# The two parts of x^T and the tile of ones allocated first in their pool

## The chip, the core and the metric

The kernel runs on one core of a Trainium2 chip. The metric is the device time of one execution in microseconds (us); the kernel before takes 1495.61 us, the median of three runs (1495.11 to 1495.95).

## What is computed

Two transformer-like blocks act on 256 tokens of width 1024, in float32. Cut to the products that matter here:

```python
def swiglu(h, wg, wu, wd):
    return (silu(h @ wg) * (h @ wu)) @ wd          # 1024 -> 2816 -> 1024

# first block: FFN, mixer (convolution + gated linear attention), FFN, embedding
h = h + 0.5 * swiglu(rmsnorm(h), ...)              # f1
z = rmsnorm(h) @ w_in                              # mixer input
h = h + concat(y_conv, y_gla) @ w_out
h = h + 0.5 * swiglu(rmsnorm(h), ...)              # f2
h = h + sigmoid(rmsnorm(h) @ w_gate) * (p @ w_proj)
# second block, two layers: FFN, attention (layer 0) or spatial gating (layer 1), FFN
x = x + g1 * swiglu(modulate(rmsnorm(x)), ...)     # f3, f5
x = x + g2 * mix(modulate(rmsnorm(x)))             # attention; spatial gating
x = rmsnorm(x + g3 * swiglu(modulate(rmsnorm(x)), ...))   # f4, f6
```

Nearly all of the arithmetic is a product of normed activations, 256 x 1024, with a weight.

## The kernel before

A float32 value is split in two float32r parts, H (a cast on ScalarE) and L (the remainder, a subtraction on VectorE). A product of two such pairs is three matmuls: H by H, L by H, H by L. The weights come from HBM as a stream of 1 MB entries, in the order of use; `Stream` issues the transfers on SP's queue, three entries ahead (tile `raw`), and splits halves of an entry into tiles `wh` and `wl`, eight of each.

The normed activations stand transposed, features on the partitions, in two tiles `xh` and `xl` of 128 partitions by 2 token tiles by 8 k-tiles by 128 tokens: 8192 bytes in each partition. `norm_T` writes them (L571 transposes, L498 and L499 split), once for each of the stages; everything that multiplies normed activations reads them. Two forms do:

- `mm3` (L490 to L492) with 128 tokens of x^T as the stationary operand and 512 columns of a weight as the moving one: the first two chunks of each FFN, and the products of the mixer, the embedding gate, attention and spatial gating. The same lines also serve the products whose stationary operand is another tile: the gated values `g` of the FFNs (`down`), and `oHL`, `sHL`, `yHL`, `cHL`, `pTHL`.
- `mmT` (L692), called by `chunkT`, with 128 columns of a weight as the stationary operand and all 256 tokens of one k-tile of x^T as the moving one, read as two runs of 128 values that lie 4096 bytes apart: the other nine chunks of each FFN and some of the mixer's input.

Every matmul loads its own stationary operand. Tile `ones_r` is the stationary operand of 18 warming products at the start (L421) and of one small sum in attention.

A list scheduler sets the order of the instructions on each engine, from priorities that the program gives (`ahead`, `spawn`, `tick`); `attention` and `sgu` set VectorE's order by hand. Memory is handed out pool by pool and, inside a pool, tile by tile in the order of the program, each tile rounded up to 32 bytes. The pool of the constants begins at byte 106,624 of each partition, a multiple of 64. Before `ones_r`, `xh` and `xl` come two tiles `h` of 4096 bytes, `kc` of 1536, `cols` of 1508 (377 columns, rounded to 1536) and `neghalf` of 32. So `ones_r`, `xh` and `xl` begin at 117,920, 118,432 and 126,624: each 32 bytes past a multiple of 64. `wh`, `wl`, `raw`, `g` and every other float32r tile begin at multiples of 64, and the slices of them that the matmuls read do too.

Of the kernel before, what the change touches and what calls it, by code (L numbers as in the profile page):

```python
# [10 lines left out]
F32R = mybir.dt.float32r  # L11
# [5 lines left out]
PSUM = bass.MemoryType.PSUM  # L17

P = 128
# [11 lines left out]
# buffers of each tag; tiles of one tag are handed out in the order of the program,  # L31
# so chains of work that run beside each other have tags of their own
# [6 lines left out]
# how many down-projection steps a tile does alone at the end of an FFN,  # L39
# and how many gate/up chunks the first tile does alone at its start  # L40
TAIL = 3
HEAD = 2
# taps of the convolution issued per us of the tensor engine's work
CONV_RATE = 3.0
# taps of each channel that the tensor engine takes
# [4 lines left out]
# how far ahead of its place in the program the scheduler may take a chain's work  # L50
# [6 lines left out]
# ---------------------------------------------------------------- weights  # L57
# Each entry of the stream is [128, 2048]: two blocks [128, 1024] of a weight.
#   "c": four k-tiles x 512 columns (two of each 1 MB entry make 8 k-tiles)
#   "d": two k-tiles x 1024 columns  # L60
#   "ada": transposed, two blocks of 128 columns of a modulation vector x 1024 rows
# [33 lines left out]
# the modulation vectors of the second block (shift, scale, gate of each part)  # L95
# are made while these FFNs run: layer, vectors
# [30 lines left out]
# columns of the packed per-partition constants  # L127
# [17 lines left out]
# columns of the shape-only constants  # L145
K_ID, K_LOW, K_UP, K_END, K_CAUSAL = 0, 128, 256, 384, 384
# rows
# [3 lines left out]
class Stream:  # L151
    """The weights, in order: DMA ahead, then split into H + L, float32r parts
    whose sum is the float32 weight."""
# [21 lines left out]
    def pump(self, now=False, n=0):  # L175
        """splits what there is room for, or n halves of an entry"""
# [38 lines left out]
class Task:  # L215
    """A chain of work given as a generator. What it yields is how much work of the
    tensor engine (us) is to be issued before the chain goes on, or a task to wait for."""
# [7 lines left out]
class Kernel:  # L225
# [25 lines left out]
    # -------------------------------------------------------------- order of issue  # L251
    @contextmanager
    def ahead(self, n):
        """the scheduler takes what is traced inside as if it were n instructions earlier"""
        tc = self.tc
        at = tc.cur_priority
        tc.cur_priority = at - n
        yield
        tc.cur_priority += n

    def pin(self, i):
        """what `after` is given later does not go before i on its engine"""
        self.pins[i.ins.engine] = i.ins
# [8 lines left out]
    def hold(self, on):  # L272
        """no weights are split while a chain runs that the tensor engine waits for"""
        self.held = on
        if not on:
            self.ws.pump()
# [31 lines left out]
    def tick(self, us):  # L308
        """so much work of the tensor engine has been issued"""
        self.pe += us  # L310
        if self.conv_q:
            self.conv_due += us * self.conv_rate
            while self.conv_q and self.conv_due >= 1.0:
                self.conv_due -= 1.0
                self.conv_q.pop(0)()
        if self.busy:
            return
        self.busy = True
        while self.heap and self.heap[0][0] <= self.pe:
            self._advance(heapq.heappop(self.heap)[2])  # L320
        self.busy = False
# [10 lines left out]
    # -------------------------------------------------------------- tiles  # L332
# [11 lines left out]
    def junk(self):  # L344
        """what only its sum is needed of"""
        return self.sp.tile([P, 512], BF16, tag="junk", name=self.nm("junk"), bufs=1)
# [7 lines left out]
    def psa(self, s, i, shape):  # L354
        """a bank of the accumulators, where none is in use"""
        return self.pacc.tile(shape, F32, tag=f"acc{i // 2}{i % 2}", name=self.nm(s))
# [10 lines left out]
    # -------------------------------------------------------------- start  # L367
    def setup(self):
        nc, a = self.nc, self.a
        self.h = [self.cpool.tile([P, D], F32, name=f"h{t}") for t in range(NT)]  # L370
# [4 lines left out]
        self.ones_r = self.cpool.tile([P, P], F32R, name="ones_r")  # L375
        nc.gpsimd.memset(self.ones_r.bitcast(F32), 1.0)
        self.xh = self.cpool.tile([P, NT, KT, P], F32R, name="xh")
        self.xl = self.cpool.tile([P, NT, KT, P], F32R, name="xl")
# [3 lines left out]
        # the first function of the scalar engine, of the table that the others here are in too  # L382
# [12 lines left out]
    def start(self):  # L395
        """x^T of the input, and the first weights"""
# [17 lines left out]
        # products of ones, that nothing reads, bring the tensor engine to its full clock  # L414
# [20 lines left out]
    # -------------------------------------------------------------- modulation  # L435
# [18 lines left out]
    def ada_end(self, layer, v, s):  # L454
        """a modulation vector: in columns, the gates in rows"""
# [30 lines left out]
    # -------------------------------------------------------------- pieces  # L486
# [8 lines left out]
    def split(self, dst, src):  # L495
        """dst = (H, L), src float32 in SBUF or PSUM"""
# [10 lines left out]
    def square(self, x, s):  # L507
        """sum of squares / 1024 of half a row"""
# [4 lines left out]
    def rstd(self, ss, t):  # L513
        """1/rms from the two halves' sums; with four, also that of 1/rms times what the other two are of"""
# [6 lines left out]
        if n == 2:  # L521
            # (s2 / (s1 + eps) + eps)^-1/2 (s1 + eps)^-1/2 = (s2 + eps (s1 + eps))^-1/2
# [6 lines left out]
    def residual(self, t, hf, gate, scale, keep):  # L529
        """h + gate * acc, half a row: in h, or keeps h"""  # L530
# [16 lines left out]
    def norm_T(self, t, ss, a, b=None):  # L547
        """x^T of tile t: (h / rms) * a + b, features on partitions, as H and L"""
# [62 lines left out]
    def finish(self, t, scale=None, gate=None, a=None, b=None, row=None, upd=None, last=False):  # L611
        """h += ..., then the norms that lead to the next x^T"""
# [38 lines left out]
    # -------------------------------------------------------------- projections  # L651
    def chunk(self, key, t, ps):
        """ps[128 tokens, 512] = x @ chunk, over 8 k-tiles"""
# [8 lines left out]
    def by_tile(self, name, cs, pss=None):  # L662
        """several chunks, all of them for one token tile before the next"""
# [6 lines left out]
    def chunkT(self, key, banks):  # L670
        """the transpose of x @ chunk: 128 columns on the partitions, all tokens;
        bank [128, 2, 256] i of the two has column blocks i and i + 2"""
# [14 lines left out]
    def mmT(self, out, w, x, first, last):  # L687
        """out[columns, tokens] += w^T x; the groups of a bank share its first start"""
# [8 lines left out]
    def down(self, t, units, first, last):  # L697
        """acc[t] += x[k-tile]^T @ weight[k-tile] over units (key, half, x)"""
# [10 lines left out]
    def down2(self, name, order, xs, fin):  # L709
        """the product with a weight of four entries: the first token tile ends early enough  # L710
        for its norms to run beside the rest of the second's"""
# [14 lines left out]
    def ffn(self, name, fin):  # L726
# [39 lines left out]
        # first chunks: a token tile at a time, so that the first need not wait for the second  # L766
# [25 lines left out]
    # -------------------------------------------------------------- first block: mixer  # L792
    def mixer_load(self):
        nc, a = self.nc, self.a
        yield 30.0
        # the 16 columns of the gate's low rank, padded to the array's width
# [15 lines left out]
    def conv_taps(self, b):  # L812
        """depthwise causal convolution of a block of channels, a tap at a time"""
# [16 lines left out]
    def conv_diag(self):  # L830
        """diagonal matrices of the last taps, for each block of channels"""
# [9 lines left out]
    def conv_pe(self, bs):  # L841
        """the last taps of some blocks of channels, as products with diagonal matrices"""
# [41 lines left out]
    def gla_gates(self, zt):  # L884
        """decays of the gated linear attention, channels on the partitions"""
# [42 lines left out]
    def gla_scores(self, banks, gates):  # L928
        """q, k with their decays; scores inside the chunks of 64; k of the chunks' end by tokens"""
# [17 lines left out]
        for t in range(NT):  # L947
# [6 lines left out]
            for e in range(2):  # L954
                # a bank for each half of the array's rows
# [12 lines left out]
    def gla_state(self, c):  # L968
        """S_{c+1} = exp(cum_end) * S_c + k_end^T v"""
# [77 lines left out]
    def mixer(self, fin):  # L1047
# [4 lines left out]
        # a * sigmoid(b): the first half of the channels a token tile at a time  # L1052
# [33 lines left out]
        # low rank of the gates  # L1086
# [56 lines left out]
    # -------------------------------------------------------------- first block: per-layer embedding  # L1143
# [37 lines left out]
    # -------------------------------------------------------------- differential attention  # L1181
    def attn_load(self):
        """bias of each head by distance, and lambda"""
# [21 lines left out]
        # lambda_init + e0 - e1, negated  # L1205
# [8 lines left out]
    def attn_qk(self, c, t, ps):  # L1214
        """q or k of four heads: rms norm of the groups of 64, channels on the partitions"""
# [22 lines left out]
    def attn_softmax(self, hf, pr, t, lane):  # L1238
        """p0 - lambda * p1 of two heads, transposed"""
# [22 lines left out]
        for i in range(2):  # L1262
            # the bias is stored from the last key to the first
# [40 lines left out]
    def attn_values(self, hf, t, deps):  # L1304
# [12 lines left out]
        # squares scaled by 2^-40; a sum beyond float32's range gives 1/rms = 0  # L1317
# [62 lines left out]
    # -------------------------------------------------------------- spatial gating  # L1380
# [84 lines left out]
    # -------------------------------------------------------------- all of it  # L1465
# [57 lines left out]
# ---------------------------------------------------------------- host: layout only  # L1523
# [6 lines left out]
def pack(inputs):  # L1530
# [21 lines left out]
    def ch(dst, parts, half):  # L1552
        # parts: column blocks of a [1024, n] weight; four k-tiles of it
# [75 lines left out]
    # bucket of the distance n - 127  # L1629
# [38 lines left out]
```

## Time and profile before

| | |
|---|---|
| device time, median of 3 | 1495.61 us |
| span of the profiled execution | 1494.0 us |
| around the span (median less span; the profiled execution's own device time is not listed apart) | 1.6 us |
| TensorE (PE) busy | 1467.5 us, 98% |
| weight loads (PEld) busy | 1300.4 us, 87% |
| VectorE (DVE), ScalarE (ACT) busy | 1086.6 and 782.3 us, 73% and 52% |
| DMA, mean | 232 GB/s |

A matmul's record runs from its start to the end of its last result, so neighbouring records overlap, and neither "busy" nor the mean of one record tells how fast matmuls follow each other. That is read from their starts: of two rows of the list in order, the difference of the start times over the number of matmuls between them. Names of operands are written out<-in; in the name of a matmul the moving operand stands first and the stationary one second.

### The profile page before, as it was taken

To read this page: it belongs to the slowest core of one execution; us is meant where nothing else is said; L and a number is where in the kernel's file an instruction comes from. 1 tells how busy PE (TensorE), PEld (TensorE's weight loads), DVE (VectorE), ACT (ScalarE), POOL (GpSimd) and SP (SyncE) were. 2 spreads that over 40 slices of the span, in tenths; PEclk is the share of its full clock that TensorE was granted. 3 is DMA by queue.
4 is the path that set the end of the run, shared out by engine and by line. 5 is a ranking of instruction groups with operands and counts; after the bars stand their busy time and mean duration, and the time that the engine had idled before them with its cause. 6 is when DMAs were issued, how large, how long until landed. Compare 5 with 4: busy or idle time off the path is not lost.

```text
span 1494.0 us, 23272 instructions
## 1 busy us (share of the span) xinstructions
PE 1467.5 (98%) x9256; PEld 1300.4 (87%) x9256; DVE 1086.6 (73%) x1693; ACT 782.3 (52%) x1238; POOL 55.2 (4%) x60
## 2 busy tenths in 40 slices
PE   8999999999999999999999999999999999999998
PEld 6999989779999878999776889998899988889997
DVE  6876569978775688775678788866987658685554
ACT  6544566265444584444586554446544455554442
POOL 1000000100000000000122100000000000000000
PEclk9999999999999999999999999999999999999999
DMA  8887544138776448786445388863899846276550
GB/s 311 335 310 267 191 149 183 64 134 319 296 290 233 148 157 320 301 315 216 155 141 199 116 330 347 325 249 127 312 350 335 300 145 235 105 291 225 205 204 29
DMA packets 52332, 346.06 MB, mean 232 GB/s; under 512 B 5912, under 2 KB 8704, under 8 KB 11776
## 3 DMA queue, kind: packets, MB, share of 16 engines
q1 hardware_dynamic: 52224, 344.58, 62.2%
q8 instruction: 72, 1.18, 0.3%
q14 instruction: 36, 0.29, 0.1%
HBM read 343.47 MB, written 1.09 MB: 231 GB/s over the span
## 4 chain that ended last, share of the span: by engine, by line
PE 80%; DVE 9%; ACT 4%; DMA 3%; issue 2%; POOL 2%; SPq 0%; POOLq 0%; DVEq 0%; ACTq 0%
PE gu L692 39%; PE acc L492 9%; PE acc L490 9%; PE acc L491 9%; DVE wl L197 4%; DMA raw<-wpack 3%; PE gu L491 2%; PE gu L492 2%; PE gu L490 2%; ACT wh L196 1%; DVE cacc L824 1%; PE xT L571 1%; POOL rn L504 1%; ACT s L1275 1%; PE cv L848 1%
## 5 line engine op out<-in xcount | busy, mean ns | idle before, releaser
L197 DVE TENSOR_TENSOR wl<-raw,wh 128x1024 fp32r<-128x1024 f32 x490 | 588.2, 1221 | 244.2 <-ACT wh L196 243.4
L196 ACT CAST wh<-raw 128x1024 fp32r<-128x1024 f32 x490 | 502.2, 1050 | 396.4 <-DMA raw<-wpack 159.4
L692 PE MATMUL gu<-xh,wh 128*128 128x256 f32 x1728 | 484.3, 281 | 1.8 <-DVE g L736 1.1
L692 PE MATMUL gu<-xl,wh 128*128 128x256 f32 x1728 | 482.2, 279 | 0.0
L692 PE MATMUL gu<-xh,wl 128*128 128x256 f32 x1728 | 482.1, 279 | 0.0
L692 PEld LDWEIGHTS gu<-xh,wh 128*128 128x128 f32 x1728 | 324.8, 188 | 5.1 <-DVE g L736 1.7
L692 PEld LDWEIGHTS gu<-xl,wh 128*128 128x128 f32 x1728 | 324.8, 188 | 2.4
L692 PEld LDWEIGHTS gu<-xh,wl 128*128 128x128 f32 x1728 | 324.8, 188 | 0.0
L492 PE MATMUL acc<-wl,g 128*128 128x512 f32 x528 | 207.2, 392 | 0.0
L490 PE MATMUL acc<-wh,g 128*128 128x512 f32 x528 | 207.2, 394 | 0.0
L491 PE MATMUL acc<-wh,g 128*128 128x512 f32 x528 | 206.5, 391 | 0.0
L447 DVE SCALAR_TENSOR_TENSOR raw<-raw,cact 128x1024 f32<-128x1024 f32 x144 | 171.7, 1219 | 17.9 <-DMA raw<-wpack 17.8
L492 PEld LDWEIGHTS acc<-wl,g 128*128 128x128 f32 x528 | 99.1, 188 | 22.4
L491 PEld LDWEIGHTS acc<-wh,g 128*128 128x128 f32 x528 | 99.1, 188 | 20.8 <-DVE g L499 1.2
L490 PEld LDWEIGHTS acc<-wh,g 128*128 128x128 f32 x528 | 99.2, 188 | 18.8
L734 ACT ACTIVATE s<-gu 128x256 f32<-128x256 f32 x108 | 40.7, 384 | 78.5 <-PE gu L692 78.3
L490 PE MATMUL gu<-wh,xh 128*128 128x512 f32 x192 | 76.7, 400 | 1.8 <-ACT wh L196 1.4
L492 PE MATMUL gu<-wl,xh 128*128 128x512 f32 x192 | 76.1, 398 | 1.4 <-DVE wl L197 1.4
L491 PE MATMUL gu<-wh,xl 128*128 128x512 f32 x192 | 76.3, 398 | 0.5 <-DVE xl L499 0.5
L736 DVE TENSOR_TENSOR g<-gu,s 128x256 f32<-128x256 f32 x108 | 44.6, 420 | 30.1 <-ACT s L734 29.5
L504 POOL TENSOR_TENSOR rn<-nv,neghalf 128x1 f32<-128x1 f32 (+1 forms) x22 | 20.1, 912 | 1244.6 <-DVE nv L518 1025.8
L498 ACT CAST g<-g 128x256 fp32r<-128x256 f32 x108 | 43.3, 407 | 38.1 <-DVE g L736 37.3
(308 smaller groups left out, 1623.6 us busy)
## 6 DMA issues: line engine op xcount, KB each, us to landing
raw<-wpack SPq DMA_DIRECT2D x316, 1024.0 KB, 4.9
gate<-grow SPq DMA_DIRECT2D x6, 512.0 KB, 4.2
row<-rows SPq DMA_DIRECT2D x5, 512.0 KB, 5.7
bias<-fd SPq DMA_DIRECT2D x16, 128.0 KB, 4.1
raw<-wpack SPq DMA_DIRECT2D x2, 512.0 KB, 7.1
out<-h SPq DMA_DIRECT2D x4, 256.0 KB, 2.2
h<-x SPq DMA_DIRECT2D x2, 256.0 KB
h<-x SPq DMA_DIRECT2D x1, 512.0 KB
```

The source lines that it names most:

```text
L196: self.last = k.after(nc.scalar.copy(out=h, in_=raw[:, u, :]))
L197: k.after(nc.vector.tensor_sub(out=l, in0=raw[:, u, :], in1=h.bitcast(F32)))
L447: self.after(nc.vector.scalar_tensor_tensor(out=raw[:, u, :], in0=raw[:, u, :], scalar=1.0, in1=self.cact, op0=ALU.mult, op1=ALU.mult, acc ...
L490: nc.tensor.matmul(out, lhsT=xh, rhs=wh, start=first, stop=False)
L491: nc.tensor.matmul(out, lhsT=xl, rhs=wh, start=False, stop=False)
L492: nc.tensor.matmul(out, lhsT=xh, rhs=wl, start=False, stop=last)
L498: self.nc.scalar.copy(out=dst[0], in_=src),
L504: self.nc.gpsimd.tensor_tensor(out=r, in0=v, in1=self.neghalf[:, :n], op=ALU.pow)
L571: self.last_T = nc.tensor.transpose(ps[:, i, :], xn[hf][:, i * P : (i + 1) * P], self.ident)
L692: nc.tensor.matmul(out, lhsT=ww, rhs=xx, start=first and n == 0, stop=last and n == 2, skip_group_check=True)
L734: nc.scalar.activation(s, b[:, 0, :], AF.Silu)
L736: nc.vector.tensor_mul(out=y, in0=b[:, 1, :], in1=s)
```

## The change

In `setup`, the three tiles are allocated first in the pool; nothing else differs but comments.

```diff
     def setup(self):
         nc, a = self.nc, self.a
+        self.xh = self.cpool.tile([P, NT, KT, P], F32R, name="xh")
+        self.xl = self.cpool.tile([P, NT, KT, P], F32R, name="xl")
+        self.ones_r = self.cpool.tile([P, P], F32R, name="ones_r")
         self.h = [self.cpool.tile([P, D], F32, name=f"h{t}") for t in range(NT)]
...
         nc.gpsimd.memset(self.neghalf, -0.5)
-        self.ones_r = self.cpool.tile([P, P], F32R, name="ones_r")
         nc.gpsimd.memset(self.ones_r.bitcast(F32), 1.0)
-        self.xh = self.cpool.tile([P, NT, KT, P], F32R, name="xh")
-        self.xl = self.cpool.tile([P, NT, KT, P], F32R, name="xl")
```

Now `xh` begins at 106,624, `xl` at 114,816 and `ones_r` at 123,008, all multiples of 64; `h` at 123,520 and 127,616, `kc` at 131,712, `cols` at 133,248 and `neghalf` at 134,784, multiples of 64 as before. From `cact` (134,816) on every address is the same, and the pools before and behind are where they were. The order of the instructions on all five engines and the semaphores that they wait for are the same, row for row, but for the numbers in the names of the tiles `h`, `xh`, `xl` and `ones_r`; no instruction is added, removed or moved, and none has another shape.

## Rows read from the trace of the kernel before

**Rows 1.** Page: engines' busy us, shares, instructions; granted clock in 40 slices.

```profile
span 1494.0 us, 23272 instructions
...
PE 1467.5 (98%) x9256; PEld 1300.4 (87%) x9256; DVE 1086.6 (73%) x1693; ACT 782.3 (52%) x1238; POOL 55.2 (4%) x60
...
PEclk9999999999999999999999999999999999999999
```

**Rows 2.** Stretches (from:to us): length, busy us (instructions) by engine, clock, DMA, GB/s.

```profile
57.30:200.00 142.70, 142.70 (x1003) 133.02 (x1004) 93.35 (x131) 73.15 (x123) 1.07 (x2) 1.00 0.67 248
850.00:1050.00 200.00, 199.05 (x1304) 180.20 (x1303) 156.68 (x228) 105.59 (x161) 2.88 (x3) 1.00 0.71 268
```

**Rows 3.** Chain of waits, first FFN's start: start us, us, what.

```profile
22.55 7.44 DMA raw<-wpack
...
57.29 0.74 PE gu L692 x4
```

**Rows 4.** Chain of waits, third FFN's start.

```profile
562.43 7.19 DMA raw<-wpack
...
573.45 7.47 DMA raw<-wpack
```

**Rows 5.** Instructions in order, PE, attention's output product: start us, us, what.

```profile
834.02 0.39 PE L492 MATMUL acc<-wl,oHL 128*128 128x512 f32 x1
...
840.89 0.39 PE L492 MATMUL acc<-wl,oHL 128*128 128x512 f32 x1
```

**Rows 6.** Instructions in order, PE, second FFN's first chunks.

```profile
324.72 0.40 PE L491 MATMUL gu<-wh,xl 128*128 128x512 f32 x1
...
329.85 0.40 PE L492 MATMUL gu<-wl,xh 128*128 128x512 f32 x1
```

**Rows 7.** Instructions in order, PE, per-layer embedding.

```profile
508.00 0.39 PE L492 MATMUL pp<-wl,pTHL 128*128 128x512 f32 x1
...
510.33 0.39 PE L490 MATMUL acc<-wh,xh 128*128 128x512 f32 x1
```

**Rows 8.** Instructions in order, PE, gate/up of the first FFN.

```profile
72.12 0.28 PE L692 MATMUL gu<-xh,wh 128*128 128x256 f32 x1
...
83.21 0.28 PE L692 MATMUL gu<-xh,wl 128*128 128x256 f32 x1
```

**Rows 9.** Instructions in order, weight loads (PEld), same place.

```profile
72.24 0.19 PEld L692 LDWEIGHTS gu<-xh,wl 128*128 128x128 f32 x1
```

**Rows 10.** Instructions in order, PE, the mixer's q and k.

```profile
230.98 0.28 PE L692 MATMUL qk<-xh,wl 128*128 128x256 f32 x1
...
240.87 0.28 PE L692 MATMUL qk<-xh,wl 128*128 128x256 f32 x1
```

**Rows 11.** Chain of waits, eight transposes in the attention stage.

```profile
845.40 0.87 PE xT L571 x8
```

**Rows 12.** Stretches, the instructions of L692 alone.

```profile
0.00:57.30 57.30, 12.17 (x97) 11.57 (x97) 1.00 0.88 323
200.00:330.00 130.00, 26.55 (x216) 25.82 (x216) 1.00 0.35 130
545.00:583.60 38.60, 12.85 (x99) 12.12 (x99) 1.00 0.79 290
...
0.00:1494.00 1494.00, 645.73 (x5400) 640.28 (x5400) 1.00 0.63 232
```

**Rows 13.** Stretches, the instructions that read or write tile xl alone.

```profile
0.00:57.30 57.30, 21.56 (x64) 12.04 (x64) 2.66 (x4) 1.00 0.88 323
200.00:330.00 130.00, 44.20 (x132) 24.82 (x132) 4.55 (x8) 1.00 0.35 130
545.00:583.60 38.60, 18.53 (x57) 10.54 (x56) 1.27 (x2) 1.00 0.79 290
742.00:850.00 108.00, 32.21 (x80) 14.93 (x80) 1.29 (x2) 1.00 0.43 154
0.00:1494.00 1494.00, 674.79 (x2232) 419.62 (x2232) 25.93 (x40) 1.00 0.63 232
```

## Prediction, before the changed kernel was run

> **What bounds the kernel now.** First the page's busy times: PE 98% of a 1494.0 us span, its weight loads 87%, the next engine 73%, and a granted clock of 9 tenths or more in every slice (1.00, the level of 2.4 GHz, in the stretches) [rows 1, 2]. Then the stretches: inside an FFN PE is busy for 142.70 of 142.70 and 199.05 of 200.00 us, while VectorE has 93 and 157, and DMA engines 0.67 and 0.71 of the time [rows 2]. So PE sets the pace, and since its records overlap, the reader must next look at the starts of single matmuls, which show how fast PE really goes. Last the chain of waits, for the places where something else sets the pace: at the start of the first FFN the chain runs over transfers of weights (7.44 us in one piece) and comes back to PE's matmuls for good at 57.29 us [rows 3]; at the start of the third it runs over transfers again (7.19 and 7.47 us) until 581 us [rows 4].
>
> **The change, part by part.** Three tiles move by addresses alone. No instruction is added, and the order is the same, so no wait, no DMA and no queue changes; `h`, `kc` and `cols` keep their place relative to 64 bytes, so I cost VectorE, ScalarE and the transfers at nothing: there is no edit of theirs to hide. What can change is how fast PE reads x^T. Two kinds of matmul read it.
>
> *x^T stationary, 512 columns of weights moving.* The trace has the same form with another stationary operand. In attention's output product, where `oHL` begins at a multiple of 64, 30 matmuls take 840.89 - 834.02 = 6.87 us, 0.2290 each [rows 5]. With x^T, 32 bytes off, 22 take 329.85 - 324.72 = 5.13 us, 0.2332 each [rows 6]. Same lines, same moving operand, same clock; the difference is 4.2 ns. Against alignment as the cause speaks `pTHL` in the embedding: a multiple of 64 too, and 10 matmuls from 508.00 to the first one with x^T at 510.33 take 0.2330 each [rows 7]. That run is short, in the middle of other work, and I take the longer run. Bounds: a gain of 0 (as `pTHL`) to 4.2 ns; I take 4.2.
>
> *x^T moving, 256 columns, weights stationary.* 95 matmuls take 83.21 - 72.12 = 11.09 us, 0.1167 each [rows 8]. That is half of the 0.2332 of rows 6 but for 0.1%: per column of the moving operand the rate is the same as in the other misaligned form (0.456 against 0.455 ns), though the one loads weights twice as often per column as the other. No row shows a 256-column matmul in float32r with an aligned x^T. From above: a loaded 128 columns of weights must still come before each; the transposes, 128 columns behind one load each, follow each other in 0.87 / 8 = 0.109 us [rows 11], so more than 7.7 ns can't be had. From below: the same operation in the mixer, x^T just as misaligned, takes (240.87 - 230.98) / 84 = 0.1177 us [rows 10], so 1.0 ns of loss between two places is possible without any change of alignment. I take the value of the nearest row, the aligned rate per column of rows 5: 0.2290 / 2 = 0.1145, a gain of 2.2 ns.
>
> *How many count.* Line 692 has 5400 matmuls [rows 12]. `xl` is read by 2232 matmuls, a third of all that read x^T with a split weight; less the 1800 of line 692, 432 are left, so the stationary form has 1296 [rows 13]. Where the chain hangs on transfers nothing is gained: up to 57.3 us 97 of the moving and 3 x (64 - 32) = 96 of the stationary form, from 545 to 583.6 us 99 and 3 x (57 - 33) = 72. In the mixer (200 to 330 us: 216 and 3 x (132 - 72) = 180) and in attention (742 to 850 us: 0 and 240) PE waits for vector work between matmuls, and I count half. That leaves 5400 - 97 - 99 - 108 = 5096 and 1296 - 96 - 72 - 90 - 120 = 918 [rows 12, 13].
>
> *Sum.* 918 x 4.2 ns = 3.9 us and 5096 x 2.2 ns = 11.2 us: 15.1 us, from a span of 1494.0 to 1478.9. What lies around the span, 1.6 us between it and the median, stays: 1480.5 us. The 18 warming products run before anything that is waited for, and are nothing. What is late next: weights. In an FFN they come with DMA engines at 0.71 and VectorE at 0.78 of the time [rows 2]; a PE that is 1% faster raises that by 0.01 each, and no new wait follows outside the two starts already left out.
>
> **A rule that speaks against it.** The weight load of each matmul takes 0.19 us in the records [rows 9], less than the 0.229 from start to start that a 512-column matmul takes [rows 5]. The Trainium skill says (TensorE: Matmul & The Clock Gate, Step-by-step: what each phase is for) that the load has an SBUF read port of its own, and that loading the next weights doesn't take bandwidth from the running matmul. By that rule the place of a hidden stationary operand costs nothing and the 3.9 us would not come. The trace disagrees as far as rows 5 and 6 go: with only the stationary operand exchanged, 4.2 ns appear.
>
> **Rivals.**
>
> *Only the stationary form gains.* Then in the moving form the weights, aligned before and after, set the pace. For it: 0.19 us of loading for 0.117 from start to start [rows 8, 9] shows loads on top of each other there. Against it: the equal rate per column of the two forms. Price: 1495.6 - 3.9 = 1491.7 us.
>
> *The moving form pays per run.* Each of its two runs of 128 values touches one 64-byte piece more when it begins in the middle of one. 512 columns at 2.4 GHz are 213.3 ns, and the aligned row has 229.0: 15.7 ns over 32 such pieces, an estimate of 0.5 ns for each, so 1.0 ns per matmul, 5.1 us. 1495.6 - 3.9 - 5.1 = 1486.6 us. For it: 18 pieces at 0.5 ns and 106.7 ns of columns come to 115.7, near the 116.7 measured. Against it: it leaves 4.2 ns for one more piece of a stationary operand.
>
> *Nothing changes.* The difference between rows 5 and 6 would be one of x^T's place or of the products around it; `pTHL` in rows 7 speaks for it: 1495.6 us. The Trainium skill would have it so (SBUF — State Buffer, Specifications (TRN2)): reads go by lines of 16 bytes, and a crossing costs. 32 and 0 past a multiple of 64 are both at the start of such a line; rows 5 and 6 differ all the same.
>
> *More.* The moving form falls towards the pace of the loads, 0.109: 5096 x 7.7 ns = 39 us, and with 3.9 us 1452.5 us at the far end. Against it: no aligned row is above 512 columns in 0.229, which is 15.7 ns over the clock.
>
> *Slower.* x^T now lies directly behind the buffers of `wl`, and both operands of every product begin at the same place of a 64-byte piece, so the two reads of PE can meet in step. In the moving form, where a load runs beside every matmul, that would show as the pace of the mixer's q and k: 1.0 ns more [rows 8, 10], 5096 x 1.0 = 5.1 us, and no gain in the stationary form: 1500.7 us. It decides from 0.8 ns on, where it eats the 3.9 us. Against it: in rows 5 both are aligned, and that is the fastest of the 512-column rows.
>
> **How the numbers follow.** Forecast 0.40 (1476 to 1484 us, with the halves of mixer and attention counted from none to all and 0.3 ns either way in the moving form); the moving form per run 0.25; only the stationary form 0.14; nothing 0.10; more 0.05; slower 0.06. The range goes from 1472 to 1493 us: from a moving form 1.5 ns better than forecast to the case of the stationary form alone and its own error; outside lie the last three, 0.21 together, of which "more" has a part inside. About 0.2%, 3.0 us, can be told from no change. Forecast, per run and more are faster (0.70), and of the stationary form alone, 3.9 us, most (0.11): 0.81. Nothing, the rest of that case and a little of the last make 0.14 within the bound; 0.05 slower.
>
> **What would show it.** In the profile after, in the list in order: 0.229 from start to start where x^T is stationary (0.233: that step is wrong); 0.1145 where it is moving (0.116: per run; 0.1167: only the stationary form; 0.118: the slow case). The mean records of lines 692 and 490 to 492 with x^T fall by those few ns, while the rows with `g` and `oHL` stay. The shares of VectorE and DMA rise by a point at most, and the start of the first FFN still ends at about 57 us. The prediction is wrong if the time stays within 3 us, or if PE's new pace is met by waits for `wh` or `wl` in the FFNs.

## The result, and the profile after

The changed kernel takes 1508.07 us, the median of 4 runs (1507.63 to 1508.98), against 1495.68 us of the kernel before, the median of 4 runs too: a ratio of 1.0084, 95% interval 1.0069 to 1.0098. It is 12.4 us slower, where 15 us less were forecast.

From the page of the changed kernel, the span, the engines' shares, the clock and the largest group of matmuls (line operation out<-moving,stationary, count, busy us and mean ns of one record):

```profile
span 1506.0 us, 23272 instructions
...
PE 1477.9 (98%) x9256; PEld 1318.1 (88%) x9256; DVE 1087.4 (72%) x1693; ACT 781.9 (52%) x1238; POOL 55.3 (4%) x60
...
PEclk9999999999999999999999999999999999999999
...
L693 PE MATMUL gu<-xh,wh 128*128 128x256 f32 x1728 | 491.3, 284 | 0.8 <-DVE g L776 0.7
```

The same group on the page of the kernel before:

```profile
L692 PE MATMUL gu<-xh,wh 128*128 128x256 f32 x1728 | 484.3, 281 | 1.8 <-DVE g L736 1.1
```

PE is as full as before, at the same clock [rows 1], but in a span of 1506.0 us instead of 1494.0. A record of the FFN's moving form (now L693) is 284 ns long on average, 3 ns more than before. Two stretches of FFN, to be held against [rows 2]:

```profile
57.30:200.00 142.70, 142.70 (x993) 133.45 (x992) 92.18 (x127) 70.71 (x118) 1.07 (x2) 1.00 0.66 245
850.00:1050.00 200.00, 199.12 (x1298) 181.88 (x1297) 153.58 (x223) 102.74 (x155) 2.31 (x3) 1.00 0.69 258
```

PE is full in both and does fewer instructions in the same time: 993 for 1003 and 1298 for 1304. DVE, ACT and DMA do less in that time, not more. So nobody makes PE wait; PE itself is slower. Where, the starts of matmuls show. In the chain of waits (start us, us, what), two neighbouring chunks of the first FFN, after the change and then before it:

```profile
105.86 11.52 PE gu L693 x96
122.88 11.50 PE gu L693 x96
```

```profile
105.72 11.21 PE gu L692 x96
122.44 11.21 PE gu L692 x96
```

96 matmuls of the moving form take 11.50 to 11.52 us, 0.1199 each, where they took 0.1167 [rows 8]. From one chunk to the next are 122.88 - 105.86 = 17.02 us; less 11.52 that leaves 5.50 us for the 24 matmuls with `g` between them, 0.229 each. Before, it was 122.44 - 105.72 - 11.21 = 5.51 us, 0.230 each: those kept their pace. And the stationary form, in the first chunks of the second FFN (instructions in order):

```profile
328.52 0.39 PE L491 MATMUL gu<-wh,xh 128*128 128x512 f32 x1
...
334.87 0.39 PE L492 MATMUL gu<-wh,xl 128*128 128x512 f32 x1
```

28 matmuls in 6.35 us, 0.2268 each, where it was 0.2332 [rows 6]. One form is 6.4 ns faster, the other 3.2 ns slower, and of the other there are four times as many. Summed from each matmul's start to that of the next on PE, the moving form went from 635.9 to 651.2 us, the stationary form from 322.5 to 318.9, the products with other stationary tiles from 443.7 to 443.0 and the rest from 82.7 to 83.5. Before rounding that is 12.0 us together, the whole of what the span grew by.

### The profile page after: what moved, and what is told of

Its sections match the earlier page's. It is cut to its first block, busy times and chain, and to the rows that moved or that the text cites. A ratio compares the mean times of both kernels' runs of the same rounds, so it can differ in the third digit from the quotient of the medians.

```text
span 1506.0 us, 23272 instructions
## 1 busy us (share of the span) xinstructions
PE 1477.9 (98%) x9256; PEld 1318.1 (88%) x9256; DVE 1087.4 (72%) x1693; ACT 781.9 (52%) x1238; POOL 55.3 (4%) x60
## 4 chain that ended last, share of the span: by engine, by line
PE 81%; DVE 9%; ACT 4%; issue 2%; POOL 2%; DMA 2%; SPq 0%; POOLq 0%; DVEq 0%; ACTq 0%
PE gu L693 40%; PE acc L493 9%; PE acc L492 9%; PE acc L491 9%; DVE wl L197 4%; PE gu L492 2%; PE gu L491 2%; PE gu L493 2%; DMA raw<-wpack 1%; PE xT L572 1%; ACT wh L196 1%; DVE cacc L825 1%; POOL rn L505 1%; ACT s L1276 1%; PE cv L849 1%
## 5 line engine op out<-in xcount | busy, mean ns | idle before, releaser
L693 PE MATMUL gu<-xh,wh 128*128 128x256 f32 x1728 | 491.3, 284 | 0.8 <-DVE g L776 0.7
L693 PE MATMUL gu<-xl,wh 128*128 128x256 f32 x1728 | 489.5, 283 | 0.0
L693 PE MATMUL gu<-xh,wl 128*128 128x256 f32 x1728 | 489.4, 283 | 0.0
L693 PEld LDWEIGHTS gu<-xh,wh 128*128 128x128 f32 x1728 | 329.1, 190 | 4.2 <-DVE g L776 1.3
L693 PEld LDWEIGHTS gu<-xl,wh 128*128 128x128 f32 x1728 | 329.1, 190 | 2.3
L693 PEld LDWEIGHTS gu<-xh,wl 128*128 128x128 f32 x1728 | 329.1, 190 | 0.0
```

The lines of the kernel that those rows point to most:

```text
L693: nc.tensor.matmul(out, lhsT=ww, rhs=xx, start=first and n == 0, stop=last and n == 2, skip_group_check=True)
```

## The experiments

Theory A, after this result: TensorE reads two operands at once, the moving one of the running matmul and the weights of the next, and the two reads meet when both begin at the same place of a 64-byte piece. That slows the moving form, in which a load runs beside every 256 columns, and not the stationary one. Rivals: B, x^T's own place in a 64-byte piece counts, whatever the weights have; C, the region of memory counts, to which x^T was moved.

### All offsets, by matmuls alone: `offset_sweep`

```python
big = pool.tile([P, 16384], F32R, name="big")       # weights and x in one tile
for v, off in enumerate((0, 8, 16, 32, 48, 64, 96, 128, 160, 192, 224, 256, 288, 384, 448, 480)):
    mmT(nm("T", v), off // 4, 0)                    # moving form, 96 matmuls: Ta, Tb, ...
    mm3(nm("S", v), off // 4, 0)                    # stationary form, 48 matmuls: Sa, Sb, ...
# Ca.. : x in one run of 256 columns at 0, 32, 64, 128
mmT("Tboth", 8, 8); mm3("Sboth", 8, 8)              # x and the weights moved by 32 bytes
mmT("Tw", 0, 8);    mm3("Sw", 0, 8)                 # the weights alone
```

> A kernel of matmuls alone (no other engine works beside them; the output is the input x and not the reference's result). Each group is 96 matmuls of the moving form (two runs of 128 columns of x, weights of 128 columns stationary) or 48 of the stationary form (128 columns of x stationary, 512 columns of weights moving), with x 0 to 480 bytes past a multiple of 512 from the weights. Theory A (both reads of TensorE meet when x and the weights begin at the same place of a 64-byte piece): moving form 0.120 us from start to start at 0, 64, 128, 192, 256, 384, 448 bytes and 0.117 at 32, 96, 160, 224, 288, 480; stationary form 0.228 and 0.233; the pair moved by 32 together like 0, the weights alone moved by 32 like 32. Theory B (x^T's own place of a 64-byte piece counts): as A, but both moved by 32 gives 0.117 and the weights alone 0.120. Theory C (where in memory x^T lies, not its place in a piece): one value at all offsets. x in one run of 256 columns: if the two runs matter, other values than with two runs at the same offset.

It ran once. Its list in order (start us, us, what, count); the pace of a group is the next group's start less its own, over its count:

```profile
25.70 11.68 PE L49 MATMUL Ta<-big 128*128 128x256 f32 x96
37.22 11.07 PE L60 MATMUL Sa<-big 128*128 128x512 f32 x48
48.13 11.85 PE L49 MATMUL Tb<-big 128*128 128x256 f32 x96
...
93.49 11.37 PE L49 MATMUL Td<-big 128*128 128x256 f32 x96
104.69 11.36 PE L60 MATMUL Sd<-big 128*128 128x512 f32 x48
115.89 11.53 PE L49 MATMUL Te<-big 128*128 128x256 f32 x96
...
229.00 11.07 PE L49 MATMUL Tj<-big 128*128 128x256 f32 x96
239.91 11.15 PE L60 MATMUL Sj<-big 128*128 128x512 f32 x48
250.89 11.52 PE L49 MATMUL Tk<-big 128*128 128x256 f32 x96
...
431.21 11.68 PE L49 MATMUL Tboth<-big 128*128 128x256 f32 x96
442.73 11.07 PE L60 MATMUL Sboth<-big 128*128 128x512 f32 x48
453.63 11.52 PE L49 MATMUL Tw<-big 128*128 128x256 f32 x96
464.99 11.36 PE L60 MATMUL Sw<-big 128*128 128x512 f32 x48
```

```
distance of x from the weights, bytes    0      8      16     32     48     64     96     128    160    192    224
moving form, us                        0.1200 0.1217 0.1188 0.1167 0.1183 0.1178 0.1198 0.1200 0.1188 0.1136 0.1183
stationary form, us                    0.2273 0.2308 0.2333 0.2333 0.2333 0.2333 0.2340 0.2333 0.2331 0.2288 0.2333
```

Ta and Sa (0 bytes) are the changed kernel's 0.120 and 0.227, Td and Sd (32 bytes) the 0.1167 and 0.233 of the kernel before: the whole effect is there with no other engine at work. Both moved (Tboth 11.52 / 96 = 0.1200, Sboth 10.90 / 48 = 0.2271) is like 0, so the distance counts and no operand's own place: B falls, and C with it. The weights alone moved by 32 put x^T at -32 bytes from them: Tw gives (464.99 - 453.63) / 96 = 0.1183, the value at 224 (256 - 32) and not that at 32, so the sign of the distance counts too. But A's rule of two values falls too. 64 and 128 bytes, in step by A, are 0.1178 and 0.1200, and at 192 bytes (Tj, Sj), also in step, the moving form is the fastest of all, 10.91 / 96 = 0.1136, with 0.2288 in the stationary form. One run of 256 columns instead of two gave 0.1199, 0.1178, 0.1178 and 0.1187 at 0, 32, 64 and 128 bytes (Ca to Cd). Without the split 0 is still the slowest of the four, so the split in two runs isn't the cause, though at 32 and 128 bytes it changes the value by some 1 ns.

### The same in the kernel: `x32_w0`, `x32_w32`, `x0_w32`

Pads of 32 bytes shift x^T, or `wh` and `wl`, or both. A pad ahead of `wh` also moves all that lies behind, so in `x0_w32` x^T, with its own pad, moves by 64 and stays at a multiple of 64. The second pad of each kernel brings everything else back to its place of 64 bytes; `g` is moved by 64 bytes in all three.

```diff
+        self.cpool.tile([P, 8], F32, name="pad_a")       # x32_w0, x0_w32
         self.xh = self.cpool.tile([P, NT, KT, P], F32R, name="xh")
...
         self.ones_r = self.cpool.tile([P, P], F32R, name="ones_r")
+        self.cpool.tile([P, 8], F32, name="pad_b")       # x32_w0, x32_w32
...
+            if not self.live and i == 0 and u == 0:      # x32_w32, x0_w32
+                k.wpool.tile([P, 8], F32, name="pad_w")
             h = k.wpool.tile([P, 1024], F32R, tag="wh", name=f"wh{i}_{u}", bufs=N_HL)
```

> The changed kernel with x^T 32 bytes further (32 past a multiple of 64, at 106,656), all else at the same place of a 64-byte piece. Theories A and B: the moving form back to 0.1167 us, the stationary form back to 0.233, the time back to that of before, 1495.7 us. Theory C (the place in memory): 0.1199 and 0.228, 1508 us.

> x^T and the split weights both 32 past a multiple of 64. Theory A: in step again, moving form 0.120 us, stationary form 0.228, about 1508 us, a few us more for the products with g, which are now out of step (0.233 for 0.229, 1894 of them, up to 7 us). Theory B: moving form 0.1167. Theory C: 0.120.

> The split weights 32 past a multiple of 64, x^T at a multiple of 64. Theory A: out of step, moving form 0.1167 us, stationary form 0.233, and with the products with g out of step too some 1496 to 1503 us. Theory B: moving form 0.120, 1508 us and up to 7 us more. Theory C: 0.120.

The chain of waits of each, two neighbouring chunks; first `x32_w0`, then `x32_w32`, then `x0_w32`:

```profile
105.26 11.20 PE gu L695 x96
121.93 11.20 PE gu L695 x96
```

```profile
105.82 11.51 PE gu L696 x96
122.93 11.51 PE gu L696 x96
```

```profile
106.14 11.20 PE gu L696 x96
122.93 11.20 PE gu L696 x96
```

With x^T alone shifted the moving form is back at 11.20 / 96 = 0.1167, and the time at 1493.10 us (ratio to before 0.9984, interval 0.9975 to 0.9994): 15 us less than the changed kernel, by 32 bytes. With both shifted it is 0.1199 again, though x^T is 32 past a multiple of 64 as in the kernel before: 1513.61 us (1.0123, 1.0107 to 1.0138). With the weights 32 past a multiple of 64 and x^T at one it is 0.1167: 1501.90 us (1.0043, 1.0028 to 1.0058). So the distance between the two operands sets the pace in the kernel as in the sweep. The 24 matmuls with `g`, from one chunk's start to the next less the 96, follow it too: (121.93 - 105.26 - 11.20) / 24 = 0.228 at the distance 0 that the pads gave it, (122.93 - 105.82 - 11.51) / 24 = 0.233 and (122.93 - 106.14 - 11.20) / 24 = 0.233 where the weights moved away by 32. By starts these products take 370.6 us in `x32_w32` against 364.8 in the changed kernel, which it exceeds by 5.5 us, and in `x0_w32` 370.1 against 365.4 in the kernel before, which it exceeds by 6.3 us: they carry all of the first difference and most of the second.

### The distance, taken at its word: `x192`, `x192_g0`, `old_place`

Theory D: the distance modulo 256 bytes sets the pace, by the sweep's table. All x^T of the kernel before stood at 32, of the changed kernel at 0; `g`, `oHL`, `sHL` and `yHL` stand at 448, which is 192 modulo 256, in both, and `pTHL` and `cHL` at 128.

```diff
 # x192: 192 bytes of small tiles ahead of x^T, taken from further behind
+        self.neghalf = self.cpool.tile([P, 8], F32, name="neghalf")
+        self.nlam = self.cpool.tile([P, 1], F32, name="nlam")
+        self.qg = self.cpool.tile([P, 1], F32, name="qg")
+        self.sg = self.cpool.tile([P, 1], F32, name="sg")
+        self.early = {n: self.cpool.tile([P, KT], F32, name=f"mod{n[0]}{n[1]}") for n in ((0, 1), (0, 0))}
         self.xh = self.cpool.tile([P, NT, KT, P], F32R, name="xh")
 # x192_g0: a pad in place of the last, so that all behind moves by 64
+        self.cpool.tile([P, 16], F32, name="pad_a")
 # old_place: the kernel before, with 32 bytes ahead of ones_r, and behind xl
+        self.cpool.tile([P, 8], F32, name="pad_a")
         self.ones_r = self.cpool.tile([P, P], F32R, name="ones_r")
```

> The changed kernel with x^T 192 bytes further (still a multiple of 64), its distance from wh and wl 192 modulo 512; four small tiles of the same pool and two modulation vectors stand ahead of it in place of a pad, so that g and all behind keep their addresses. Theory A: in step by 64 bytes, 0.120 us for the moving form, 1508 us. Theory D: 0.1133 and 0.229, so from the 1495.6 us of before 5400 x 3.4 ns = 18 us and 1296 x 4.3 ns = 6 us less, of which some 22 arrive: 1473 us.

> As x192, with the pools behind moved by 64 bytes, so that g, oHL, sHL and yHL stand at distance 0 from the weights. Theory D: the products with g at 0.2275 instead of 0.229 (1894 x 1.6 ns = 3 us), 1470 us. Theory A: 1508 us and no gain with g.

> The kernel before with 32 bytes more ahead of ones_r, xh and xl: they stay at their old place and begin at multiples of 64 (distance 64 from the weights, and g at distance 0). Theory A: 0.120 and 0.228, about 1505 us. Theory D: 0.1178 and 0.2333, and g at 0.2275: 1495.6 + 5400 x 1.1 ns - 1894 x 1.6 ns = 1498.5 us. Theory C (place in memory): 1495 us or less.

`x192`, two neighbouring chunks in the chain of waits, and the stationary form in order:

```profile
104.53 10.91 PE gu L697 x96
120.93 10.91 PE gu L697 x96
```

```profile
327.01 0.39 PE L495 MATMUL gu<-wh,xh 128*128 128x512 f32 x1
...
332.27 0.39 PE L497 MATMUL gu<-wl,xh 128*128 128x512 f32 x1
```

The moving form is at 10.91 / 96 = 0.1136, the stationary one at (332.27 - 327.01) / 23 = 0.2287: the values of the sweep at 192 bytes, at an address that is a multiple of 64 like the changed kernel's. The time is 1478.54 us, 16.5 us under the kernel before (0.9891, interval 0.9876 to 0.9906): faster than both kernels. Some 22 were expected. By starts the moving form gave its 15.7 us (635.9 to 620.2) and the stationary form only 2.2 (322.5 to 320.3). Of the 1296 matmuls with x^T stationary, the starts that lie under 0.3 us apart went from a mean of 0.2333 (1200 of them) to 0.2294 (1195), a gain of 4.7 us, and the longer ones grew from 42.4 to 46.2 us in sum. More than half of that gain was so given back in waits, and not all of the moving form reached the fast pace, as the next section shows.

`old_place`, the same view:

```profile
104.60 11.31 PE gu L694 x96
121.39 11.31 PE gu L694 x96
```

0.1178, the sweep's value at 64 bytes, and 1497.49 us (1.0017, 1.0007 to 1.0026), where A said 1505 and D 1498.5: a multiple of 64 at the old place is no better than what was there. `x192_g0`:

```profile
104.32 11.31 PE gu L697 x96
121.07 11.31 PE gu L697 x96
```

Here D missed. The products with `g` came to (121.07 - 104.32 - 11.31) / 24 = 0.2267, as expected, but the moving form, at the same 192 bytes, to 0.1178; 1491.35 us (0.9977, 0.9968 to 0.9987) instead of 1470.

### One distance, two paces: `offset_sweep2` and `offset_sweep3`

```python
# offset_sweep2: every 32 bytes of 512, stationary form first; then 192 and 448 behind a group in step
for v in range(16):
    mm3(nm("S", v), v * 8, 0); mmT(nm("T", v), v * 8, 0)
for v in (6, 14):
    for r in "xyz":
        mm3(nm("A", v) + r, 0, 0); mmT(nm("R", v) + r, v * 8, 0, 8 if r == "y" else 32)
# offset_sweep3
for r in "xyz":
    mm3("Aj" + r, 48, 0); mmT("Fj" + r, 48, 0)      # behind 192 bytes
    mm3("Aa" + r, 0, 0);  mmT("Gj" + r, 48, 0)      # behind 0 bytes
# Pall, Pxh, Pxl, Pwh, Pwl: all parts in step, then one of them 32 bytes away
# Ba..Bh: the moving form in bfloat16 at 0, 32, ... 224 bytes
```

> Matmuls alone again (the output is the input x and not the reference's result): x every 32 bytes from 0 to 480 past a multiple of 512 from the weights, each offset first in the stationary form and then in the moving form; then 192 and 448 three times in the moving form behind 48 matmuls that are in step. Theory D (the distance of the two operands modulo 256 sets the pace): each offset gives the value of the first sweep (moving: 0.120 at 0, 0.1167 at 32, 0.1178 at 64, 0.120 at 96 and 128, 0.1187 at 160, 0.1133 at 192, 0.1183 at 224 bytes; stationary: 0.2267 at 0, 0.2289 at 192, 0.2333 elsewhere) and the same again from 256 on, 448 like 192. Against it stands 0.1178 at 448 in the first sweep: if that repeats, the distance counts modulo 512; if 448 now gives 0.1133 or the three repetitions differ, the pace depends on what ran before, too. Theory A (place in a 64-byte piece): two values only.

> Matmuls alone (the output is the input x and not the reference's result). First: at distance 192 the moving form behind 48 matmuls of the stationary form at 192 (Fj, three times) and behind 48 at distance 0 (Gj, three times). Theory E (two stable paces at 192, and what runs before picks one): Fj 0.1133, Gj 0.1178, each three times. Theory D alone (distance): all six 0.1133. Second: the moving form with all four parts in step (Pall 0.120) and then one of them 32 bytes away. If the running matmul's moving read meets the load of the next matmul's weights, Pxh changes the runs of two moving reads in three and Pxl of one, Pwh the loads of two in three and Pwl of one, and all four lie between 0.1167 and 0.120, Pxh and Pwh nearer to 0.1167; if the pace hung on x^T's or on the weights' own place, only the two of its kind would change. Third: the moving form in bfloat16, every 32 bytes of 256: if two bytes per column ask half as much of the reads, one pace at all offsets, near the 0.107 us that 256 columns take at 2.4 GHz; if the meeting of the reads costs the same there, a spread like float32r's, 6 ns.

`offset_sweep2` in order, 448 bytes behind its own stationary form (So, To), and 192 behind a group at distance 0 (Rgx):

```profile
341.23 11.15 PE L53 MATMUL So<-big 128*128 128x512 f32 x48
352.21 11.07 PE L42 MATMUL To<-big 128*128 128x256 f32 x96
363.12 11.36 PE L53 MATMUL Sp<-big 128*128 128x512 f32 x48
...
396.61 11.47 PE L42 MATMUL Rgx<-big 128*128 128x256 f32 x96
407.91 11.04 PE L53 MATMUL Agy<-big 128*128 128x512 f32 x48
```

The sixteen offsets gave eight values, each at 256 bytes more again; 448, 0.1178 in the first sweep, is now 10.91 / 96 = 0.1136 like 192. So the period is 256 bytes. Not every value is that of the first sweep, though: 160 bytes gave 0.1173 for 0.1188, and 384 bytes, 0.1188 in the first sweep, gave the 0.1200 of 128. And behind a group at distance 0, 192 bytes gave (407.91 - 396.61) / 96 = 0.1177, all three times, and 448 too. That is the case of `x192_g0`, whose moving form runs behind products with `g` at distance 0. `offset_sweep3` in order:

```profile
36.42 11.07 PE L43 MATMUL Fjx<-big 128*128 128x256 f32 x96
47.33 11.06 PE L54 MATMUL Aax<-big 128*128 128x512 f32 x48
...
80.54 11.47 PE L43 MATMUL Fjy<-big 128*128 128x256 f32 x96
91.84 11.04 PE L54 MATMUL Aay<-big 128*128 128x512 f32 x48
...
158.53 11.68 PE L67 MATMUL Pall<-big 128*128 128x256 f32 x96
170.04 11.48 PE L67 MATMUL Pxh<-big 128*128 128x256 f32 x96
181.36 11.40 PE L67 MATMUL Pxl<-big 128*128 128x256 f32 x96
192.59 11.48 PE L67 MATMUL Pwh<-big 128*128 128x256 f32 x96
203.91 11.52 PE L67 MATMUL Pwl<-big 128*128 128x256 f32 x96
215.27 10.65 PE L79 MATMUL Ba<-half 128*128 128x256 bf16 x96
225.76 10.64 PE L79 MATMUL Bb<-half 128*128 128x256 bf16 x96
```

The first moving group behind 192 bytes is fast (10.91 / 96 = 0.1136), but the second, Fjy, behind the same stationary group, is not (11.30 / 96 = 0.1177), nor was the third; the three behind distance 0 are all slow. So there are two stable paces at 192 bytes, but theory E's rule, that the group just before picks one, holds only one way: behind distance 0 it was slow each time, behind 192 it was either. What picks is open.

The traces of the two kernels, by starts, lean the way of theory E. Each has 66 unbroken runs of 12 or more matmuls of the moving form. In `x192`, with `g` at 192 bytes, all 48 that follow products with `g` are fast, with means of 0.1135 to 0.1147; in `x192_g0`, with `g` at 0, 47 of these 48 are at 0.1178. Of the 18 that follow anything else, 10 are fast in `x192` and 11 in `x192_g0`. A run of 75 near the end, behind a single transpose, is even slow in the first and fast in the second; in the chains of waits of `x192` and then `x192_g0`:

```profile
1394.67 8.84 PE gu L697 x75
```

```profile
1406.91 8.53 PE gu L697 x75
```

It is 8.84 / 75 = 0.1179 in the first and 8.53 / 75 = 0.1137 in the second.

At distance 0, 0.1199 (Pall); with any one of the four parts 32 bytes away, 0.1179, 0.1170, 0.1179 and 0.1183. Moving either side of the pair makes it faster, so both sides count. The order expected among the four, from which reads would meet, didn't come. In bfloat16 the eight offsets are one value, 10.49 / 96 = 0.1093 (Ba, against Bb at 225.76; the other seven 0.1091 to 0.1092): there the distance costs nothing. Its weight loads are shorter too, by its page (mean ns of one record after the busy us):

```profile
L79 PEld LDWEIGHTS <-half 128*128 128x128 bf16 x768 | 75.0, 98 | 8.7
```

98 ns is less than the pace of its matmuls, while the loads of float32r take 188 to 192 ns for 114 to 122 from start to start. So this run doesn't tell whether the narrower reads or the shorter loads make the distance harmless.

## Why the prediction was wrong

*What bounds the kernel* was right: the change is in PE's own pace, and VectorE, ScalarE and the transfers stayed hidden but for a few us of waits. *How many count* was near for the moving form: 15.3 us at 3.2 ns each are some 4800 matmuls, for 5096.

*The stationary form*: 3.9 us of gain forecast, 3.6 measured by starts. That it came so near is luck. The starts that lie under 0.3 us apart came 5.2 ns sooner by mean (0.2333 for 1200 of them, 0.2281 for 1197), some 6 us in all, and the longer ones grew from 42.4 to 45.9 us in sum. The cause under it was wrong. Rows 5 and 6 differ by the distance of the stationary tile from the weights, 448 bytes (192 modulo 256) against 32, not by a multiple of 64. `pTHL` in rows 7, named as the evidence against, was the counterexample: aligned, at distance 128, 0.2330, where the sweep has 0.2333.

*The moving form* is the step that failed: "I take the value of the nearest row, the aligned rate per column of rows 5: 0.2290 / 2 = 0.1145, a gain of 2.2 ns". It became 0.1199, a loss of 3.2 ns; 5096 x 3.2 ns = 16.3 us, less 3.6, makes 12.7 us for the 12.4 measured. The equal rate per column of the two forms at distance 32, on which the step leaned, is a coincidence of that offset: at 0 they are 0.469 and 0.444 ns per column, at 192 they are 0.444 and 0.447.

*The rivals.* The slower one, at a chance of 0.06, had the direction of the moving form. Its rule, the same place of a 64-byte piece, fell with the sweep, the two reads that it names are not shown, and the stationary form, for which it foresaw no gain, gained 3.6 us. Its price of 1.0 ns came from the mixer's q and k [rows 10]; the sweep has 3.3 between 32 bytes and 0. Those rows were a second pace at one distance: in the kernel before the 122 matmuls of that run go at 0.1178 from beginning to end, with x^T 32 bytes off as everywhere. The other sentence against it, that rows 5 are aligned and the fastest, took aligned for in step: `oHL` is 192 bytes off. "Per run" would have had the moving form gain, and the one-run columns of the sweep kept the loss. "More" was half right: 0.1136 can be had, by another distance.

*The rule* of the Trainium skill (TensorE: Matmul & The Clock Gate, Step-by-step: what each phase is for), that the weight load has its own read port and takes nothing from the running matmul, was set aside on a difference of 4.2 ns. In bfloat16 the sweep agrees with it: 0.1092 at every offset. The Trainium skill (TensorE: Matmul & The Clock Gate, Back-to-back issue gap) gives for an isolated matmul of 256 columns an estimate of 256 / 2.4 + 2.5 = 109.2 ns, which is that value. In float32r the rule doesn't foresee what was measured: 0.1136 to 0.1217 with nothing but the distance changed.

## What to carry to other kernels

In a product in float32r like this one, compare the distance between the addresses of the two operands before each one's own alignment; an address that looks clean can be the slow one. A pace seen for one form of an operation says little about the other form, in which the operands change roles; a sweep of matmuls alone, one short run, gave a table whose paces five of the six kernels showed; three of the six were planned with it, and three from it. And the row that contradicts a rule drawn from two others should be priced as the rule's failure, not as noise.

## What the runs showed of the hardware

At full clock (1.00 granted throughout the three sweeps), matmuls in float32r with a weight load each follow each other at a pace that depends on the distance of x^T from the weights, modulo 256 bytes: 0.1136 to 0.1217 us with 256 columns, 0.227 to 0.234 us with 512. No distance tried is best for both forms: 0 gives 0.1200 and 0.2273, 192 gives 0.1136 and 0.2288. The distance isn't all: at 192 the moving form has a second stable pace, 0.1177, at 32 the kernel before has runs at 0.1178 beside 0.1167, and what picks is open. In bfloat16 the moving form with 256 columns has one pace at all eight distances. That the load of the next weights is what the moving read meets is inferred from this and was not shown by itself.
